# Moving the second layer's modulations out of the mixer, a transposed inverse, and six buffers in place of three

## The chip, the core and the metric

One core of a Trainium2 chip runs the whole program. The metric is the device time of one execution in microseconds (us); the time of a kernel is the median over its runs.

## What is computed

A backbone over 256 latent tokens and 256 context tokens of 1024 channels, with two layers. The first mixes tokens by a gated DeltaNet and differential attention, the second by a 2-D Fourier transform; each is followed by a PEER mixer (128 x 128 product keys, 16384 experts). Cut to what the change touches:

```
for i in range(DEPTH):                                        # DEPTH 2
    mod = (silu(c) @ ada_w[i] + ada_b[i]).reshape(bsz, 6, 1, D_MODEL)
    sh1, sc1, g1, sh2, sc2, g2 = (mod[:, j] for j in range(6))
    h = rmsnorm(x, norm1_w[i]) * (1.0 + sc1) + sh1
    if i % 2 == 0:
        y = mixer_ab(h, h_c, ...)   # h_c: the context, normalised and modulated alike
    else:
        y = fourier_mix(h) @ w_out_f[j]
    x = x + g1 * y
    x = x + g2 * peer(rmsnorm(x, norm2_w[i]) * (1.0 + sc2) + sh2, ...)
return rmsnorm(x, final_norm_w)

def gated_delta_chunked(...):      # in mixer_ab, per chunk of 64 tokens, head and direction
    m = where(strict, einsum('nbhid,nbhjd->nbhij', kb, kc) * decay, 0.0)
    t_inv = triangular_solve(eye + m, eye, lower=True, unit_diagonal=True)

def peer(h, w_q, sub_keys, u_tab, v_tab):
    ...                            # top 16 of the keys per head, softmax gates
    act = gelu(h . u_tab[idx]);  out = sum((gate * act) * v_tab[idx])
```

So layer 1's `mod` (six vectors of 1024, out of a 1024 x 6144 matrix) depends on `c` alone, and is first needed after peer 0.

## The kernel before

**The stages.** The mixer of layer 0 runs from the start to about 470 us, then peer 0, the Fourier layer, and peer 1 with the last norm. In the mixer, 29 products with the tiles of the input projection come first (17 of all 512 columns, context and latent tokens together, then 12 of the latent tokens' 256 columns), and each product's result is handed to a task (`do_k`, `do_ba`, `do_v`, `do_bk`, `do_bv`, `do_bq`, `do_q`, `do_gate`; list at L1318). The scalars of the DeltaNet (`do_ba` leads to `scalars`, L850, and `triangles`, L920) and the keys give 64 x 64 triangles `M`; `inverse` (L956) inverts the two diagonal 32 x 32 blocks of each, row by row, for 128 triangles at once (one on each partition). `blocks` (L1001) transposes the inverse `X` to the layout of the later steps, `merge` (L1029) adds the off-diagonal corner, `scan` runs the chunks in order. `attend` is the attention, in units of a score product, a softmax and a product with the values.

**The order.** `Lanes` (L50) records every instruction and plans it itself: the program is written as generators that yield at waits, a greedy planner keeps a cost for each operation (`took`, L98) and issues on each engine in the order in which the generators become ready. Each engine then runs its instructions strictly in that order. All instructions are therefore shown under one line, L133.

**Weights.** `Stream` (L200) carries all weight tiles of the program, 128 x 1024 f32 (512 KB) each, in one fixed order: `loads` (L214) issues them on SP's DMA queue into one of three `raw` buffers, and `cuts` (L225) splits a tile into two halves of reduced precision: ACT copies raw to `hi`, DVE computes `lo` = raw - hi. Buffers for the pairs are `pair` (two pairs), and, by stage, `wide` and `h` lent to the stream. `mm3` (L275) forms a product as hi.x_hi + hi.x_lo + lo.x_hi, 24 matmuls a tile. A matmul on f32 data shows as two records in the trace, one on the fp32r pairs as one.

**Peer.** 16 tiles of `wq`, 128 of `u` and 128 of `v`. While the first u tiles are multiplied, DVE selects the top keys and `weigh` (L1616) writes the gates; the u tiles after that and all v tiles have DVE and ACT for the cuts and for the splitting of the gated activations alone.

**Modulations.** `modulations` in the mixer (L579) goes over six parts (`parts`, L569), three of each layer, each of 16 chunks of `ada_w` (512 KB, `mraw` buffers, on SP's queue as well). A chunk's step is 4 matmuls (32 columns stationary, 256 moving, shown as 8 records); after each part a row copy, 4 transposes and one addition on DVE follow. Parts 0 to 2 are layer 0's, parts 3 to 5 layer 1's. `start` (L654) makes the modulated context and latent tokens: for each of 8 blocks POOL computes the context's `h` and the difference `h - hi`, DVE those of the latent tokens.

Of the kernel before, what the change touches and what calls it, by code (L numbers as in the profile page):

```python
# [9 lines left out]
F32 = mybir.dt.float32  # L10
# [4 lines left out]
OP = mybir.AluOpType  # L15
# [4 lines left out]
KC = 8  # L20
# [2 lines left out]
NEG = -3.0e38  # L23
GSC = 32768.0
SKEW = 16
AHEAD = 6
SUMMED = 6
LN_EXP = "natural_log_exp_and_others"
# [21 lines left out]
class Lanes:  # L50
# [149 lines left out]
class Stream:  # L200


    def __init__(self, c, pool, sources):
        self.c, self.n, self.sources = c, 0, sources
        lanes = c.nc
        self.raws = lanes.stock([c.t(pool, [128, 1024], tag=f"raw{i}") for i in range(3)])
# [18 lines left out]
    def cuts(self):  # L225
        for n in range(len(self.sources)):
            yield self.loaded[n]
            raw, t = self.raw.pop(n)
            hi = yield from self.parts[0].take()
            yield t  # L230
            self.c.nc.scalar.activation(hi, raw, AF.Copy)
            yield
            lo = yield from self.parts[1].take()
            self.tile[n] = hi, lo
            self.c.nc.vector.tensor_tensor(lo, raw, hi.bitcast(F32), op=OP.subtract)
            self.raws.give(raw)
            self.cut[n].set()
            yield

    def next(self):  # L240
        n = self.n
        self.n += 1
        yield self.cut[n]
        return self.tile.pop(n)
# [10 lines left out]
class Ctx:  # L255


    def __init__(self, tc, es, sources):
# [6 lines left out]
        self.stream = Stream(self, self.const, sources)  # L265

    def t(self, pool, shape, dt=F32, tag=None, **k):
        self.n += 1
# [269 lines left out]
def mixer(c, xT, aff, g1, coming, A):  # L538


    with ExitStack() as es:
# [24 lines left out]
        flight = lanes.stock(range(3))  # L566


        parts = [(i, p) for i in range(2) for p in range(3)]  # L569
        modk = events(len(parts))  # L570
        mrow = new([128, 512], tag="mrow")
        mraw = [new([128, 4, 256], tag=f"mraw{i}") for i in range(2)]
        mraw = [[view(S3, 4, 256, at=i * 1024) for i in range(4)] + mraw] + [mraw] * 5

        there = lanes.event()
        fetched = {n: lanes.event() for n in (6, 16)}
# [77 lines left out]
        def start():  # L654
# [21 lines left out]
            for n, k in enumerate(first):  # L676
                if n % 4 == 0:
                    yield mod0[n // 4]
                    (sc, shc), (s1, sh1) = (aff(r, n // 4) for r in (1, 0))
                for x, lo, eng, scale, shift in ((ctxT, 0, nc.gpsimd, sc, shc), (xT, NT, nc.vector, s1, sh1)):  # L680
                    hi = hb[:, 0, k, lo:lo + NT]
                    h = yield from hs.take()
                    nc.scalar.activation(hi, x[:, k], AF.Identity, scale=scale[:, k:k + 1], bias=shift[:, k:k + 1])
                    eng.tensor_scalar(h, x[:, k], scale[:, k:k + 1], shift[:, k:k + 1], op0=OP.mult, op1=OP.add)
                    eng.tensor_tensor(hb[:, 1, k, lo:lo + NT], h, hi.bitcast(F32), op=OP.subtract)
                    hs.give(h)
                hk[k].set()
            nc.gpsimd.memset(kbd, 0.0)
# [267 lines left out]
        def inverse():  # L956
            nc.gpsimd.memset(X, 0.0)
            nc.gpsimd.memset(S4[:, 0:4096:65], 1.0)
            yield
            Xb = [X[:, b * 32:b * 32 + 32, b * 32:b * 32 + 32] for b in range(2)]  # L960
            Mb = [M[:, b * 32:b * 32 + 32, b * 32:b * 32 + 32] for b in range(2)]
            for i in range(1, 32):
                for b in range(2):
                    nc.vector.tensor_tensor(pr[:, b, :i, :i], Mb[b][:, i, :i].unsqueeze(1).broadcast_to([128, i, i]),
                                            Xb[b][:, :i, :i].rearrange("p j x -> p x j"), op=OP.mult)
                for b in range(2):
                    nc.vector.tensor_reduce(Xb[b][:, i, :i], pr[:, b, :i, :i], axis=AX.X, op=OP.add)
                yield
            Xk.set()

# [30 lines left out]
        def blocks(d):  # L1001
            yield [Xk, zk]
            T = late["T"]
            ln = slice(d * 64, d * 64 + 64)
            for b in range(8):
                ps = yield from banks.take()
                pt = ps[:64].rearrange("p (x h u) -> p x h u", x=8, h=2)
                for a in range(8):
                    i = b * 8 + a
                    nc.tensor.transpose(pt[:, a], X[ln, :, i] if d else X[ln, i, :], c.ident[ln, ln])  # L1010
                yield
                for hp, q in halves():
# [302 lines left out]
                yield  # L1315


        tasks = [(do_k, p, 512) for p in range(4)] + [(do_ba, 0, 512)] + [(do_v, p, 512) for p in range(4)]  # L1318
        tasks += [(do_bk, p, 512) for p in range(4)] + [(do_bv, p, 512) for p in range(4)]
        tasks += [(do_bq, p, NT) for p in range(4)] + [(do_q, p, NT) for p in range(4)]  # L1320
        tasks += [(do_gate, p, NT) for p in range(4)]
# [74 lines left out]
def peer(c, layer, xT, shift, g2, coming, A):  # L1396
# [3 lines left out]
    with c.tc.tile_pool(name=f"peer{layer}", bufs=1) as dp:  # L1400
# [6 lines left out]
        a1 = c.t(dp, [128, 1024], F16, tag="a1")  # L1407
        x = c.scaled
        squares, c.squares = c.squares, Squares(c, layer == 0)
        late = {}  # L1410

        def region(j, n):
# [327 lines left out]
def trunk(tc, A, out):  # L1740
    with ExitStack() as es:
        tiles = lambda *names: [a[i] for a in names for i in range(a.shape[0])]
        layers = [tiles(A["wq"][i], A["u"][i], A["v"][i]) for i in range(2)]
        c = Ctx(tc, es, tiles(A["w_in"], A["w_out_ab"]) + layers[0] + [A["dft"]] + tiles(A["w_out_f"])
                + layers[1])
        nc = c.nc

        def const(name):
# [51 lines left out]
def arrays(i):  # L1800
# [17 lines left out]
    a["ada_w"] = con(i["ada_w"].reshape(2, 8, 128, 3, 4, 2, 256).transpose(0, 3, 5, 1, 2, 4, 6)).reshape(2, 3, 2, 8, 128, 1024)  # L1818
# [14 lines left out]
    a["w_in"] = np.concatenate([tiles(ak), tiles(ba), tiles(av), tiles(bk), tiles(bv), tiles(bq), tiles(aq), tiles(ag)])  # L1833
    a["conv"] = con(i["conv_w"][0].reshape(3, 12, 128).transpose(2, 1, 0))

    def lanes(x):
# [52 lines left out]
```

## Time and profile before

| what | value |
|---|---|
| runs | 2110.34, 2113.05 (median), 2118.28 us |
| profiled execution | 2115.18 us |
| its span | 2113.4 us |
| granted TensorE clock, mean | 0.989 |

The profile is of one execution. The span runs from the first to the last instruction of the trace. PE is the matmul engine and PEld its weight loads, DVE the vector engine, ACT the scalar engine, POOL GpSimd, SP the engine whose queue issues the loads. Names in rows are the program's: `S` holds the modulated tokens of the mixer, `bank` is a PSUM bank, `area` is shared storage of the mixer (`X` of the inverse lies in it), and `wide<-h,area` is the inverse's product row (`pr` in `wide`, `M` in `h`).

### The profile page before, as it was taken

What the parts mean: (1) busy time and instruction counts of PE and PEld (TensorE: products, weight loads), DVE (VectorE), ACT (ScalarE), POOL (GpSimd) and SP (SyncE); (2) the same over time, 40 slices, a digit from 0 to 9 for tenths busy, and PEclk for the clock granted to TensorE, in tenths of its full rate; (3) what the DMA queues carried; (4) which work ended last, traced back from release to release, by engine and by line L of the source; (5) the groups of instructions that cost most, each with busy time, mean ns of one, the idle gap of its engine ahead of it and who ended that gap; (6) DMA issues with size and microseconds to landing.
All of it is one profiled execution on the core that took longest, in us unless ns stands there. A gap on an engine that the chain in (4) does not pass through costs nothing.

```text
span 2113.4 us, 43065 instructions
## 1 busy us (share of the span) xinstructions
PE 2063.5 (98%) x17732; PEld 1933.9 (92%) x17732; DVE 1549.2 (73%) x3039; ACT 1022.1 (48%) x1542; POOL 82.8 (4%) x122
## 2 busy tenths in 40 slices
PE   7999989999999999999999999999999999999998
PEld 3566658989999999999999989999999999999997
DVE  3479978879998999565555556999899956555554
ACT  4443344155545444554444545554544455444453
POOL 3000023000000000000000000000000000000000
PEclk8999999999999999999999999999999999999999
DMA  7655671045565444665655543556544466666553
GB/s 300 213 180 169 232 240 38 1 133 180 189 198 170 142 149 151 198 212 196 192 195 194 193 160 116 172 190 199 170 141 149 150 199 211 195 194 193 196 192 118
DMA packets 102549, 370.65 MB, mean 175 GB/s; under 512 B 11696, under 2 KB 12976, under 8 KB 101968
## 3 DMA queue, kind: packets, MB, share of 16 engines
q1 hardware_dynamic: 102352, 367.90, 53.0%
q8 instruction: 138, 2.26, 0.4%
q14 instruction: 59, 0.48, 0.1%
HBM read 366.71 MB, written 1.15 MB: 174 GB/s over the span
## 4 chain that ended last, share of the span: by engine, by line
PE 79%; DVE 10%; DMA 6%; ACT 3%; issue 1%; POOL 0%; SPq 0%; POOLq 0%; ACTq 0%; DVEq 0%
PE bank L133 79%; DMA raw<-in_u_dram 3%; DVE wide_lo L133 3%; DVE pair L133 2%; DVE wide L133 2%; DMA mraw<-in_ada_w_dram 2%; DVE DD L133 1%; DVE area L133 1%; ACT pair L133 1%; DMA area<-in_ctx_dram 1%; ACT wide L133 0%; ACT DD L133 0%; DMA area<-in_ada_w_dram 0%; ACT bank L133 0%; DVE a L133 0%
## 5 line engine op out<-in xcount | busy, mean ns | idle before, releaser
L133 ACT ACTIVATE pair<-raw 128x1024 fp32r<-128x1024 f32 x376 | 399.1, 1062 | 435.2 <-PE bank L133 342.9
L133 DVE TENSOR_TENSOR pair<-raw,pair 128x1024 fp32r<-128x1024 f32 x376 | 458.1, 1219 | 182.8 <-ACT pair L133 167.1
L133 PE MATMUL bank<-h,pair 128*128 128x256 f32 x4464 | 557.4, 280 | 0.0
L133 PEld LDWEIGHTS bank<-h,pair 128*128 128x128 f32 x4464 | 528.8, 188 | 0.2 <-DVE pair L133 0.2
L133 PE MATMUL bank<-wide,pair 128*128 128x256 f32 (+1 forms) x3456 | 417.1, 277 | 0.0
L133 PEld LDWEIGHTS bank<-wide,pair 128*128 128x128 f32 x3456 | 405.4, 188 | 0.6
L133 PE MATMUL bank<-wide,h 128*128 128x256 f32 x2880 | 336.6, 276 | 0.0
L133 PEld LDWEIGHTS bank<-wide,h 128*128 128x128 f32 x2880 | 331.3, 188 | 0.0
L133 PE MATMUL bank<-h,wide 128*128 128x256 f32 x2160 | 264.5, 277 | 0.0
L133 PEld LDWEIGHTS bank<-h,wide 128*128 128x128 f32 x2160 | 253.7, 188 | 0.0
L133 DVE TENSOR_TENSOR h<-raw,h 128x1024 fp32r<-128x1024 f32 x120 | 147.0, 1225 | 140.1 <-ACT h L133 140.1
L133 ACT ACTIVATE h<-raw 128x1024 fp32r<-128x1024 f32 x120 | 127.4, 1062 | 161.8 <-PE bank L133 149.2
L133 PE MATMUL bank<-S,pair 128*128 128x256 f32 (+1 forms) x888 | 195.5, 362 | 4.2 <-POOL S L133 2.5
L133 PEld LDWEIGHTS bank<-S,pair 128*128 128x128 f32 x888 | 138.8, 199 | 52.3 <-issue 29.9
L133 ACT ACTIVATE DD<-bank 128x512 f32<-128x512 f32 (+25 forms) x284 | 107.6, 394 | 95.8 <-PE bank L133 92.8
L133 ACT ACTIVATE wide<-raw 128x1024 fp32r<-128x1024 f32 x90 | 95.6, 1062 | 106.7 <-PE bank L133 53.3
L133 DVE TENSOR_TENSOR wide<-raw,wide 128x1024 fp32r<-128x1024 f32 x90 | 109.3, 1214 | 2.3 <-ACT wide L133 2.0
L133 DVE TENSOR_TENSOR wide<-DD,wide 128x512 fp32r<-128x512 f32 x128 | 87.3, 684 | 8.3 <-ACT wide L133 8.2
L133 DVE TENSOR_TENSOR DD<-bank,DD 128x512 f32<-128x512 f32 (+13 forms) x84 | 42.3, 504 | 64.8 <-ACT bank L133 61.2
L133 DVE TENSOR_TENSOR wide_lo<-wide_lo,pT 128x1024 f16<-128x1024 f16 x128 | 85.9, 681 | 0.0
L133 ACT ACTIVATE wide<-DD 128x512 fp32r<-128x512 f32 x128 | 78.6, 615 | 9.5 <-PE bank L133 9.5
L133 POOL TENSOR_TENSOR wide_lo<-wide_lo 128x256 f32<-128x256 f32 x10 | 8.3, 834 | 1591.5 <-ACT wide_lo L133 1590.9
(242 smaller groups left out, 1893.7 us busy)
## 6 DMA issues: line engine op xcount, KB each, us to landing
raw<-in_u_dram SPq DMA_DIRECT2D x256, 512.0 KB, 3.5
raw<-in_v_dram SPq DMA_DIRECT2D x256, 512.0 KB, 4.3
mraw<-in_ada_w_dram SPq DMA_DIRECT2D x84, 512.0 KB, 4.2
raw<-in_wq_dram SPq DMA_DIRECT2D x32, 512.0 KB, 3.5
raw<-in_w_in_dram SPq DMA_DIRECT2D x29, 512.0 KB, 4.3
area<-in_ada_w_dram SPq DMA_DIRECT2D x12, 512.0 KB, 6.3
raw<-in_w_out_ab_dram SPq DMA_DIRECT2D x8, 512.0 KB, 4.5
raw<-in_w_out_f_dram SPq DMA_DIRECT2D x8, 512.0 KB, 3.5
```

Of the source, the lines that this page charges most:

```text
L133: return f(*args, **kw)
```

## The change

Five parts.

1. Layer 1's modulations leave the mixer: `parts` is three long there. Their 48 chunks, re-cut to 128 x 1024 (`ada_late`), go through the stream instead, one behind every third of the last 150 tiles of layer 0 (22 of u and all 128 of v of peer 0). DVE adds each chunk, scaled by the activated conditioning, into `acc`; after 8 chunks 8 matmuls with `acc` as the stationary operand and a column of ones as the moving one sum it over the partitions, and DVE adds the bias.
2. The stream has six raw buffers, not three, and the program a smaller scratch for DMA descriptors.
3. In `start`, the context's `h - hi` of the last four blocks goes from POOL to DVE.
4. `inverse` treats both 32 x 32 blocks in one operation, so it issues 31 products and 31 sums where it issued 62 and 62; X is kept transposed, so that the product reads X along adjacent elements instead of 64 elements (256 bytes) apart. `blocks` transposes the other one of its two cases.
5. `do_ba` is the first task, so the scalars come before the keys.

```
+RAW = 6
+ADA = 1, 0, 2, 4, 3, 5
 class Stream:
-        self.raws = lanes.stock([... for i in range(3)])
+        self.raws = lanes.stock([... for i in range(RAW)])
     def cuts(self):
             raw, t = self.raw.pop(n)
+            if n in self.sums:
+                yield from self.sum(raw, t, *self.sums[n])
+                continue
+    def sum(self, raw, t, m, k):
+        nc, w = self.c.nc, self.c.cact[:, k, 0:1]
+        if k == 0 and m != ADA[0]:
+            yield self.read[ADA[ADA.index(m) - 1]]
+        yield t
+        if k == 0:
+            nc.vector.tensor_scalar(self.acc, raw, w, None, op0=OP.mult)
+        else:
+            nc.vector.scalar_tensor_tensor(self.acc, raw, w, self.acc, op0=OP.mult, op1=OP.add)
+        self.raws.give(raw)
+        if k == KC - 1:
+            self.summed[m].set()
+        yield
+    def modulations(self):
+        for m in ADA:
+            yield self.summed[m]
+            ps = yield from c.banks.take()
+            for j in range(8):
+                nc.tensor.matmul(ps[:, j:j + 1], self.acc[:, j * 128:j * 128 + 128], c.ones[:, :1], start=True, stop=True)
+            self.read[m].set()
+            yield
+            nc.vector.tensor_tensor(c.mod[1][:, 0, m * 8:m * 8 + 8], ps[:, :8], c.adab[:, 1, m * 8:m * 8 + 8], op=OP.add)
+            c.banks.give(ps)
 def mixer(...):
-        parts = [(i, p) for i in range(2) for p in range(3)]
+        parts = [(0, p) for p in range(3)]
-        mraw = [[view(S3, 4, 256, at=i * 1024) for i in range(4)] + mraw] + [mraw] * 5
+        mraw = [[view(S3, 4, 256, at=i * 1024) for i in range(4)] + mraw] + [mraw] * 2
     def start():
-                    eng.tensor_tensor(hb[:, 1, k, lo:lo + NT], h, hi.bitcast(F32), op=OP.subtract)
+                    (eng if n < 4 else nc.vector).tensor_tensor(hb[:, 1, k, lo:lo + NT], h, hi.bitcast(F32), op=OP.subtract)
     def inverse():
-            for i in range(1, 32):
-                for b in range(2):
-                    nc.vector.tensor_tensor(pr[:, b, :i, :i], Mb[b][:, i, :i].unsqueeze(1).broadcast_to([128, i, i]),
-                                            Xb[b][:, :i, :i].rearrange("p j x -> p x j"), op=OP.mult)
-                for b in range(2):
-                    nc.vector.tensor_reduce(Xb[b][:, i, :i], pr[:, b, :i, :i], axis=AX.X, op=OP.add)
+            for i in range(1, 32):
+                x = both(X[:, 0, 0:1], [64, i], [1, i])
+                p = pr[:, :, :i, :i]
+                nc.vector.tensor_tensor(p, both(M[:, i, 0:1], [0, i], [1, i]), x, op=OP.mult)
+                nc.vector.tensor_reduce(both(X[:, 0, i:i + 1], [64, i]), p, axis=AX.X, op=OP.add)
     def blocks(d):
-                    nc.tensor.transpose(pt[:, a], X[ln, :, i] if d else X[ln, i, :], c.ident[ln, ln])
+                    nc.tensor.transpose(pt[:, a], X[ln, i, :] if d else X[ln, :, i], c.ident[ln, ln])
-        tasks = [(do_k, p, 512) for p in range(4)] + [(do_ba, 0, 512)] + [(do_v, p, 512) for p in range(4)]
+        tasks = [(do_ba, 0, 512)] + [(do_k, p, 512) for p in range(4)] + [(do_v, p, 512) for p in range(4)]
 def peer(c, layer, ...):
+        if layer == 0:
+            stream.acc = c.t(dp, [128, 1024], tag="acc")
+            lanes.add(stream.modulations())
 def trunk(tc, A, out):
+        chunks = [(m, k) for m in ADA for k in range(KC)]
+        sources, sums = tiles(A["w_in"], A["w_out_ab"]) + layers[0][:-150], {}
+        for j, v in enumerate(layers[0][-150:]):
+            sources.append(v)
+            while len(sums) < len(chunks) and j >= 3 * len(sums):
+                m, k = chunks[len(sums)]
+                sums[len(sources)] = m, k
+                sources.append(A["ada_late"][m, k])
 def kernel(**inputs):
+    nc = bacc.Bacc(..., dynamic_dma_scratch_size=1024)
```

`both(a, ...)` is an access pattern with a leading dimension of 2 blocks, 32 x 65 elements apart; the host's array of `w_in` tiles has the tile of `do_ba` first.

The planned order changes with it. **PE, the first narrow products of the mixer** (`S,pair` is a product with a tile of the input projection, `mraw,cact` a chunk's step, `area,bq` a score). Before:

```order
L133 MATMUL bank_4_67<-S_38_117,pair_15_78 128x256 x8
L133 MATMUL bank_3_66<-mraw_36_115,cact_88 32x256 x4
L133 MATMUL bank_8_71<-S_38_117,pair_12_75 128x256 x4
L133 MATMUL bank_5_68<-bq_120,later_138 128x256
L133 MATMUL bank_8_71<-S_38_117,pair_12_75 128x256 x4
L133 MATMUL bank_3_66<-mraw_37_116,cact_88 32x256 x4
L133 MATMUL bank_8_71<-S_38_117,pair_12_75 128x256 x8
L133 MATMUL bank_8_71<-S_38_117,pair_13_76 128x256 x8
L133 MATMUL bank_6_69<-area_28_107,bq_120 128x512
```

After:

```order
L135 MATMUL bank_1_64<-S_41_120,pair_18_81 128x256 x8
L135 MATMUL bank_6_69<-S_41_120,pair_15_78 128x256 x8
L135 MATMUL bank_5_68<-bq_123,later_141 128x256
L135 MATMUL bank_6_69<-S_41_120,pair_15_78 128x256 x8
L135 MATMUL bank_6_69<-S_41_120,pair_16_79 128x256 x8
L135 MATMUL bank_7_70<-S_41_120,pair_17_80 128x256 x4
L135 MATMUL bank_2_65<-bq_123,later_141 128x256
L135 MATMUL bank_7_70<-S_41_120,pair_17_80 128x256 x12
L135 MATMUL bank_7_70<-S_41_120,pair_18_81 128x256 x8
```

No step of a chunk stands between the products any more. By this order, 9 of layer 1's 48 steps stood among the wide products, 29 among the narrow ones and 10 behind them. Of the 16 score products 11 stood before the end of the narrow products and 5 behind; now it is 8 and 8.

**DVE, the end of the inverse** (`wide<-h,area` is the row product, `area<-wide` the sum, `sm`, `qT` and `bq` belong to the attention and the queries). Before:

```order
L133 TENSOR_REDUCE sm_136<-bank_3_66 128x1
L133 SCALAR_TENSOR_TENSOR area_31_110<-area_31_110,later_138 128x256
L133 TENSOR_SCALAR sm_136<-sm_136 128x1
L133 TENSOR_TENSOR wide_112<-h_111,area_29_108 128x31x31
L133 SCALAR_TENSOR_TENSOR area_31_110<-area_31_110,later_138 128x256
L133 TENSOR_TENSOR wide_112<-h_111,area_29_108 128x31x31
L133 TENSOR_REDUCE area_29_108<-wide_112 128x31 x2
L133 TENSOR_TENSOR pair_13_76<-raw_11_74,pair_12_75 128x1024
L133 TENSOR_REDUCE sm_136<-bank_4_67 128x1
```

After:

```order
L135 TENSOR_REDUCE sm_139<-bank_6_69 128x1
L135 TENSOR_SCALAR area_34_113<-area_34_113,later_141 128x256
L135 TENSOR_SCALAR sm_139<-sm_139 128x1
L135 TENSOR_TENSOR wide_115<-h_114,area_32_111 128x2x31x31
L135 SCALAR_TENSOR_TENSOR area_34_113<-area_34_113,later_141 128x256
L135 TENSOR_REDUCE area_32_111<-wide_115 128x2x31
L135 SCALAR_TENSOR_TENSOR area_34_113<-area_34_113,later_141 128x256
L135 TENSOR_TENSOR pair_18_81<-raw_14_77,pair_17_80 128x1024
```

Two products and two sums of a row became one of each, over both blocks; the rest of the queue around them is the same kind of work. Of the 29 cuts of the input projection's tiles, the 17th stood behind row 19 of the inverse and the 27th behind the last row, 31; now the 17th stands behind row 22 and the 24th behind row 31.

**PE, peer 0 where the value tiles begin** (`h,pair` is a product of a u tile, `wide,pair` one of a v tile). Before there were only these products here; in the change the first of six such groups stands among them:

```order
L135 MATMUL bank7_8_71<-h_73_3505,pair00_15_78 128x256 x16
L135 MATMUL bank7_8_71<-h_73_3505,pair01_16_79 128x256 x8
L135 MATMUL bank7_8_71<-h_73_3505,pair10_17_80 128x256 x8
L135 MATMUL bank5_6_69<-ones_22_87,acc_76_3508 128x1 x8
L135 MATMUL bank7_8_71<-h_73_3505,pair10_17_80 128x256 x8
L135 MATMUL bank7_8_71<-h_73_3505,pair11_18_81 128x256 x8
```

and on DVE, there, the bias addition (`mod1`) stands ahead of the next chunk's sum and the next cut:

```order
L135 TENSOR_TENSOR pair01_16_79<-raw3_12_75,pair00_15_78 128x1024
L135 TENSOR_TENSOR mod1_26_94<-bank5_6_69,early_20_83 128x8
L135 TENSOR_SCALAR acc_76_3508<-raw0_9_72,cact_24_91 128x1024
L135 SCALAR_TENSOR_TENSOR s11_79_12638<-mod1_26_94,early_20_83 128x8
L135 TENSOR_TENSOR pair11_18_81<-raw4_13_76,pair10_17_80 128x1024
```

The six groups are added; nothing was taken out of these two queues at this place.

## Rows read from the trace of the kernel before

**Rows 1.** The page, its busy times (part 1) and the chain that ended last (part 4).

```profile
PE 2063.5 (98%) x17732; PEld 1933.9 (92%) x17732; DVE 1549.2 (73%) x3039; ACT 1022.1 (48%) x1542; POOL 82.8 (4%) x122
...
PE 79%; DVE 10%; DMA 6%; ACT 3%; issue 1%; POOL 0%; SPq 0%; POOLq 0%; ACTq 0%; DVEq 0%
```

**Rows 2.** Windows: from:to, length, busy (x) of PE, PEld, DVE, ACT, POOL, clock, DMA, GB/s.

```profile
35.00:205.50 170.50, 166.94 (x1015) 106.41 (x1016) 115.81 (x252) 72.95 (x122) 20.12 (x16) 0.96 0.56 189
205.50:298.80 93.30, 85.23 (x619) 56.97 (x619) 78.30 (x138) 38.95 (x84) 11.43 (x14) 0.93 0.69 233
298.80:332.30 33.50, 29.36 (x290) 18.54 (x291) 29.39 (x61) 18.45 (x42) 10.51 (x2) 1.00 0.58 182
...
690.70:841.50 150.80, 148.57 (x1458) 144.80 (x1457) 143.36 (x227) 73.80 (x140) 0.00 (x0) 1.00 0.45 145
850.00:1240.00 390.00, 390.00 (x3440) 390.00 (x3439) 218.44 (x217) 192.12 (x218) 0.00 (x0) 1.00 0.60 194
```

**Rows 3.** Windows, tile mraw: PE, PEld busy, then clock, DMA, GB/s.

```profile
205.50:298.80 93.30, 19.41 (x232) 4.76 (x232) 0.93 0.69 233
298.80:332.30 33.50, 6.39 (x80) 1.57 (x80) 1.00 0.58 182
```

**Rows 4.** Timeline of PE in the mixer: start, duration, operation, [idle before <-releaser].

```profile
41.58 1.65 PE L133 MATMUL bank<-S,pair 128*128 128x512 f32 x3 [2.51 <-POOL S L133]
...
188.28 0.64 PE L133 MATMUL bank<-mraw,cact 128*32 128x256 f32 x8 [0.47 <-DMA mraw<-in_ada_w_dram]
...
203.19 0.64 PE L133 MATMUL bank<-mraw,cact 128*32 128x256 f32 x8
203.75 1.78 PE L133 MATMUL bank<-S,pair 128*128 128x512 f32 x9
...
276.72 1.08 PE L133 MATMUL bank<-mraw,cact 128*32 128x256 f32 x8 [2.53 <-DMA mraw<-in_ada_w_dram]
...
298.69 1.12 PE L133 MATMUL bank<-area,bq 64*128 64x512 f32 x2
```

**Rows 5.** DVE by line: all forms of the inverse's two operations, and single shapes.

```profile
L133 DVE TENSOR_TENSOR wide<-h,area 128x1 f32<-128x1 f32 (+30 forms) x62 | 44.8, 747 | 0.1
L133 DVE TENSOR_REDUCE area<-wide 128x1 f32<-128x1 f32 (+30 forms) x62 | 28.6, 491 | 0.0
...
L133 DVE TENSOR_TENSOR wide<-h,area 128x961 f32<-128x961 f32 x2 | 3.8, 1910 | 0.0
...
L133 DVE TENSOR_REDUCE area<-wide 128x31 f32<-128x961 f32 x2 | 2.2, 1180 | 0.0
```

**Rows 6.** DVE by line: a contiguous subtraction, and a scaled addition of 512 elements.

```profile
L133 DVE TENSOR_TENSOR pair<-raw,pair 128x1024 fp32r<-128x1024 f32 x376 | 458.1, 1219 | 182.8 <-ACT pair L133 167.1 <-PE bank L133 11.9 <-issue 3.5
...
L133 DVE SCALAR_TENSOR_TENSOR wide_lo<-wide_lo,sm 128x512 f32<-128x512 f32 x8 | 6.0, 747 | 0.1
```

**Rows 7.** Windows: the DMA engines at full load.

```profile
20.00:40.00 20.00, 15.45 (x102) 7.01 (x101) 12.58 (x34) 12.76 (x25) 11.78 (x14) 0.75 1.00 388
```

**Rows 8.** Timeline of PE: stationary 128 columns with few moving columns.

```profile
335.73 1.50 PE L133 MATMUL bank<-area 128*128 128x128 f32 x12
...
1265.95 0.50 PE L133 MATMUL bank<-ones,wide_lo 128*128 128x1 f32 x4
1266.32 0.48 PE L133 MATMUL bank<-pair,h 128*128 128x512 f32 x1
```

**Rows 9.** Waits in the stretch 690.7 to 841.5: who, for whom, us, times, longest.

```profile
ACT pair L133 <- DMA raw<-in_u_dram: 15.6, 13, 2.2
ACT wide L133 <- DMA raw<-in_u_dram: 13.9, 9, 2.8
DVE DD L133 <- ACT bank L133: 5.6, 10, 1.1
```

**Rows 10.** Timeline of PE: a u tile in peer 0 after the gates.

```profile
846.96 2.88 PE L133 MATMUL bank<-h,wide 128*128 128x256 f32 x24
849.68 5.60 PE L133 MATMUL bank<-h,pair 128*128 128x256 f32 x48
```

More of the change, by code (lines that the diff above doesn't have):

```diff
@@ L200, with __init__ @@
 class Stream:
-    def __init__(self, c, pool, sources):
-        self.c, self.n, self.sources = c, 0, sources
+    def __init__(self, c, pool, sources, sums):
+        self.c, self.n, self.sources, self.sums = c, 0, sources, sums
+        self.order = [n for n in range(len(sources)) if n not in sums]
+        self.acc, self.summed, self.read = None, c.nc.events(6), c.nc.events(6)
         lanes = c.nc
-        self.raws = lanes.stock([c.t(pool, [128, 1024], tag=f"raw{i}") for i in range(3)])
+        self.raws = lanes.stock([c.t(pool, [128, 1024], tag=f"raw{i}") for i in range(RAW)])
         self.parts = [lanes.stock(x) for x in zip(*(c.pair_tiles(pool, f"pair{i}") for i in range(2)))]
@@ L238, in cuts @@
             yield
+    def sum(self, raw, t, m, k):
[12 more added lines that the diff above has]
+    def modulations(self):
+        c, nc = self.c, self.c.nc
+        for m in ADA:
[7 more added lines that the diff above has]
+            c.banks.give(ps)
     def next(self):
-        n = self.n
+        n = self.order[self.n]
         self.n += 1
@@ L255, with __init__ @@
 class Ctx:
-    def __init__(self, tc, es, sources):
+    def __init__(self, tc, es, sources, sums):
         self.tc, self.nc = tc, Lanes(tc.nc)
@@ L264, in __init__ @@
         self.banks = self.nc.stock([self.t(banks, [128, 512], tag=f"bank{i}") for i in range(8)])
-        self.stream = Stream(self, self.const, sources)
+        self.stream = Stream(self, self.const, sources, sums)
     def t(self, pool, shape, dt=F32, tag=None, **k):
@@ L959, in inverse, with both @@
             yield
-            Xb = [X[:, b * 32:b * 32 + 32, b * 32:b * 32 + 32] for b in range(2)]
-            Mb = [M[:, b * 32:b * 32 + 32, b * 32:b * 32 + 32] for b in range(2)]
+            def both(a, *ap):
+                return bass.AP(tensor=a.tensor, offset=a.offset, ap=[a.ap[0], [32 * 65, 2], *ap])
             for i in range(1, 32):
-                for b in range(2):
-                    nc.vector.tensor_tensor(pr[:, b, :i, :i], Mb[b][:, i, :i].unsqueeze(1).broadcast_to([128, i, i]),
-                                            Xb[b][:, :i, :i].rearrange("p j x -> p x j"), op=OP.mult)
-                for b in range(2):
-                    nc.vector.tensor_reduce(Xb[b][:, i, :i], pr[:, b, :i, :i], axis=AX.X, op=OP.add)
+                x = both(X[:, 0, 0:1], [64, i], [1, i])
+                p = pr[:, :, :i, :i]
+                nc.vector.tensor_tensor(p, both(M[:, i, 0:1], [0, i], [1, i]), x, op=OP.mult)
+                nc.vector.tensor_reduce(both(X[:, 0, i:i + 1], [64, i]), p, axis=AX.X, op=OP.add)
                 yield
@@ L1743, in trunk @@
         layers = [tiles(A["wq"][i], A["u"][i], A["v"][i]) for i in range(2)]
-        c = Ctx(tc, es, tiles(A["w_in"], A["w_out_ab"]) + layers[0] + [A["dft"]] + tiles(A["w_out_f"])
-                + layers[1])
+        chunks = [(m, k) for m in ADA for k in range(KC)]
[6 more added lines that the diff above has]
+                sources.append(A["ada_late"][m, k])
+        c = Ctx(tc, es, sources + [A["dft"]] + tiles(A["w_out_f"]) + layers[1], sums)
         nc = c.nc
@@ L1816, in arrays @@
     a["cc"] = con(np.stack([i["c"][0], i["c_ctx"]], -1).reshape(8, 128, 2).transpose(1, 0, 2))
-    a["ada_w"] = con(i["ada_w"].reshape(2, 8, 128, 3, 4, 2, 256).transpose(0, 3, 5, 1, 2, 4, 6)).reshape(2, 3, 2, 8, 128, 1024)
+    a["ada_w"] = con(i["ada_w"][:1].reshape(1, 8, 128, 3, 4, 2, 256).transpose(0, 3, 5, 1, 2, 4, 6)).reshape(1, 3, 2, 8, 128, 1024)
+    a["ada_late"] = con(i["ada_w"][1].reshape(8, 128, 6, 1024).transpose(2, 0, 1, 3))
     a["ada_b"] = con(i["ada_b"].reshape(2, 48, 128).transpose(2, 0, 1))
@@ L1832, in arrays @@
     ba = np.concatenate([rows(bt), rows(al)] * 4, 1)
-    a["w_in"] = np.concatenate([tiles(ak), tiles(ba), tiles(av), tiles(bk), tiles(bv), tiles(bq), tiles(aq), tiles(ag)])
+    a["w_in"] = np.concatenate([tiles(ba), tiles(ak), tiles(av), tiles(bk), tiles(bv), tiles(bq), tiles(aq), tiles(ag)])
     a["conv"] = con(i["conv_w"][0].reshape(3, 12, 128).transpose(2, 1, 0))
@@ L1879 @@
     host = arrays({k: np.asarray(v) for k, v in inputs.items()})
-    nc = bacc.Bacc("TRN2", target_bir_lowering=False, num_devices=1)
+    nc = bacc.Bacc("TRN2", target_bir_lowering=False, num_devices=1, dynamic_dma_scratch_size=1024)
     A = {k: nc.dram_tensor(f"in_{k}_dram", v.shape, mybir.dt.from_np(v.dtype), kind="ExternalInput").ap()
```

## The prediction, made before the changed kernel ran

> **What bounds the kernel now.** I read the page first: PE is busy 98% of the span and the chain that ended last lies 79% on PE, 10% on DVE, 6% on DMA [rows 1]. So most of the program goes at PE's pace, and a gain is either PE work taken out or one of the few stretches in which PE waits. The windows by stage [rows 2] show them. In the plain u and v tiles of peer 0 (850 to 1240) PE is busy for all 390 us, DVE for 218, ACT for 192, and the loads run at 194 GB/s. In the stretch where the gates are written (690.7 to 841.5) DVE is busy 143.4 of 150.8 us and PE 148.6. In the mixer there are three stretches: the wide products (35 to 205.5, PE 166.9 of 170.5), the narrow ones (205.5 to 298.8, PE 85.2 of 93.3 at a clock of 0.93, DVE 78.3), and the rest of the attention up to the first merge (298.8 to 332.3, PE 29.4 of 33.5). Times are summed against the profiled execution, 2115.2 us; the median of the runs is 2.1 lower.
>
> **1. The chunks leave the mixer.** Of their 48 steps in layer 1, 9 stood among the wide products, 29 among the narrow ones, 10 behind. A step takes PE 0.57 us: 203.19 to the next product's start at 203.75 [rows 4]; the windows of this tile agree in count, 232 records for 29 steps of 8 and 80 for 10 [rows 3].
>
> *Wide products.* DVE is busy for 115.8 of 170.5 us there [rows 2], so what is added to it (four differences, of some 0.4 us, and the earlier inverse) is covered. PE's gain: 9 x 0.57 = 5.1, and most of one wait of 2.51 us on POOL's `S` at 41.58 [rows 4], since four differences leave POOL; that wait can give between 0 and 2.5, and I take 2, as POOL's own scalings ahead of it stay. With the wait of 0.47 us for a chunk at 188.28 [rows 4], **−7.5**.
>
> *Narrow products.* Here two engines have to give way at once. PE: 29 x 0.57 = 16.5, two groups of four transposes of a row (8 at 0.09, as the cheapest of rows 8: 0.7), one wait of 2.53 us for a chunk [rows 4], and three score products of 1.1 us each [rows 4], which now stand behind the last product: 3.3. That is 23. DVE: the inverse is 44.8 + 28.6 = 73.4 us in all [rows 5]. It computes 2 x (1 + 4 + ... + 961) = 20832 products; those of 961 took 1.91 us, that is 1.9 to 2.0 ns each, and their sum 1.18 us, 1.1 to 1.2 each [rows 5]. A cut, on adjacent elements, takes 1219 / 1024 = 1.19 ns [rows 6]. Reading X along adjacent elements, I put a product at 1.1 (that is 1.19 less the fixed part, some 0.08 us an instruction), a sum at 1.1 as before, and half as many fixed parts: 2 x 20832 x 1.1 ns = 46 and 62 x 0.08 = 5, 51 us in place of 73. Behind the 17th cut, DVE's order held the rows from 20 on, 15892 products at 1.9 + 1.1 ns and their fixed parts, some 50 us; it now holds those from 23 on, 13242 at 1.1 + 1.1, some 30. So DVE falls by about 20 and by 1 or 2 for softmaxes that move behind the products. The stretch follows the lesser of the two and keeps its idle time: **−22**.
>
> No row separates what X's stride costs from what the broadcast operand costs. From above it is 1.9 ns a product, the rate of rows 5; from below 1.1 as in rows 6; I take the latter, the same kind of operation on f32. [...]
>
> *Behind the products.* 10 x 0.57 = 5.7, four transposes 0.4, and about 1 of PE's 4.1 idle us [rows 2] are gone; the three score products come with 3.3 and what waits behind their softmaxes, of which I let 2 us show: **−2** (−7 to +8, the upper end with all of a unit's chain uncovered).
>
> **2. The chunks arrive in peer 0.** *PE.* 48 matmuls, 96 records, of 128 stationary columns and one moving column. The nearest rows: with one moving column 4 records took 0.37 us to the next start (1265.95 to 1266.32), 0.09 each; with 128 moving columns 12 took 1.50, 0.125 each [rows 8]. Between these, 0.11: 96 x 0.11 = 10.6 us (8.9 to 12.0), on the path, because PE is full there [rows 2]. The 48 steps taken away had cost 27. [...]
>
> *The first addition.* DVE's queue holds `mod1`, the next chunk's sum and then the next cut. `mod1` waits for the 16 records behind which PE has one more product half (16 matmuls, 1.8 us by rows 10) and a whole tile (2.72 us) before it needs that cut; DVE needs about 0.2 + 1.3 + 0.2 + 1.2 = 2.9. It can be late only when the cut's own ACT copy is: 0 to 1.4 us, and I take 1.4. The other five groups stand among v tiles with the same lead. Together **+12**.
>
> *DVE and DMA.* A sum of 1024 elements costs between 1.22 (the cut) and 1.49 us (twice 747) [rows 6]: 48 x 1.3 = 62 us, over 390 + 12 us of which DVE has 171 free [rows 2]. That cover fails only where DVE's lead over PE is used up. The loads: 48 more of 512 KB bring 194 to about 252 GB/s, and the queue has carried 388 for 20 us [rows 7]. Nothing.
>
> **3. Six raw buffers.** While the gates are written, ACT stands 15.6 + 13.9 = 29.5 us before `raw` loads that were issued too late, because a buffer comes free only when DVE has made the difference [rows 9]. Its queue then delays DVE (DVE waits for ACT 5.6 us in 10 pieces [rows 9]). DVE's 143.4 us of work is a floor, PE's own is lower: 42 tiles at 2.72 us [rows 10] and the transposes of the gates, some 142. With 150.8 us of time the gain is at most 7, at least nothing, if DVE's waits on ACT come from PE's results and not from the loads. I take 4, in the middle, and as the stretch comes in both peers, **−8** (0 to −14).
>
> **Sum.** −7.5 − 22 − 2 + 12 − 8 = −27.5; 2115.2 − 27.5 = 2087.7, and 2.1 lower for the median: **2086 us**, 1.3% faster.
>
> **Rivals.** A measurement of this kernel can tell a change of 0.5% (10.6 us) from none.
> - *A, the stride was not the price* (0.10). If products still cost 1.9 ns, DVE keeps 11 us in the narrow products, and the later start of what hangs on the inverse another 2 to 4: they gain some 8 instead of 22. Time: about 2100. For it: the broadcast operand remains; against: the contiguous cut.
> - *B, the attention's tail becomes the bound* (0.10). The score products moved behind the last product each start a chain over DVE and ACT; if these 8 units instead of 5 run without cover, the third stretch is 10 us longer instead of 2 shorter: about 2098.
> - *C, slower* (0.03). Each of the 48 sums stands ahead of a cut in DVE's queue. If the cuts are made just in time, each sum holds the next tile by its 1.3 us: +62 in place of nothing, 2148. It decides when DVE's lead is below one tile; against it stands the 44% of idle time of DVE while PE never waits [rows 2].
> - *D, more than I count* (0.09). The idle 8 us and the slow clock of the narrow products (0.93) both vanish, and both gate stretches reach DVE's floor: 2068.
> - *E, three buffers were enough* (inside the main case). ACT's waits turn out to be covered: 8 us less gain, 2094.
>
> **How the numbers follow.** The main case, 2074 to 2096, has 0.68: its bounds are 0 to −14 for the buffers and 8.9 to about 20 for peer 0. With A, B and D the range reaches 2066 to 2101; what lies outside is C, the worse half of A and the better half of D. Faster by over 0.5% is below 2102.5: the main case, B, D and most of A, 0.91; within 0.5%: 0.06; slower 0.03.
>
> **What would show it.** Among narrow products no wait for `mraw`, the stretch some 71 us long. One row product of the inverse over 2 x 961 elements near 2.1 us (A: 3.7). Peer 0's plain tiles 402 us long instead of 390, PE without idle time, 96 records of 0.1 us, and DVE 280 us busy (C: waits of PE for `pair`). The gate stretches near 147, with no wait of ACT for `raw`. The prediction is wrong if PE waits in peer 0 for DVE, or if the first merge does not come about 30 us earlier.

## The result and the profile after

The changed kernel's runs took 2086.86, 2089.08 and 2094.13 us, a median of 2089.08; those of the kernel before on the same chips have a median of 2115.66. The ratio is 0.9877 (95% interval 0.9856 to 0.9897), 1.2% faster, 26.6 us by the medians. The profiled execution took 2089.08 us, 26.1 less than that of before. (A fourth run, of 2527.46 us at a granted clock of 0.747, is left out.)

The page's busy times, against [rows 1]: PE lost 30 us of busy time and DVE gained 37.5.

```profile
PE 2033.6 (97%) x17432; PEld 1931.1 (93%) x17432; DVE 1586.7 (76%) x3032; ACT 1020.9 (49%) x1539; POOL 84.2 (4%) x118
```

Windows by stage, in the columns of [rows 2]: the wide products, the narrow ones, the rest up to the first merge, the stretch of the gates in peer 0. The last row is peer 0 from the same u tile as 860.6 in the kernel before to the first Fourier product; there that took 396.3 us.

```profile
36.00:194.40 158.40, 157.57 (x944) 104.23 (x945) 117.67 (x213) 73.34 (x122) 16.47 (x11) 0.99 0.53 179
194.40:258.60 64.20, 58.70 (x372) 47.11 (x372) 59.03 (x100) 34.27 (x75) 12.51 (x15) 0.95 0.38 115
258.60:293.40 34.80, 25.47 (x204) 16.76 (x200) 29.40 (x68) 18.76 (x46) 10.13 (x2) 0.80 0.05 16
...
651.30:798.50 147.20, 147.12 (x1458) 144.37 (x1457) 143.64 (x228) 75.09 (x141) 0.00 (x0) 1.00 0.46 150
...
817.60:1234.80 417.20, 409.99 (x3579) 407.99 (x3578) 274.58 (x283) 195.49 (x228) 0.73 (x1) 1.00 0.73 245
```

Laid side by side by the start of the same PE instructions in both traces, the difference is: up to the narrow products −11.5 us, the narrow products −29.2, behind them to the first merge +1.8, the rest of the mixer and the first u tiles −0.5, gates of peer 0 −3.6, peer 0 from there +20.9, the Fourier layer −1.0, gates of peer 1 −3.5; the rest is within 0.6. The sum is −26.2.

DVE by line, against [rows 5]: the inverse's products and sums, all forms and the largest.

```profile
L135 DVE TENSOR_TENSOR wide<-h,area 128x2 f32<-128x2 f32 (+30 forms) x31 | 26.5, 855 | 0.6
L135 DVE TENSOR_REDUCE area<-wide 128x2 f32<-128x2 f32 (+30 forms) x31 | 26.3, 849 | 0.5
...
L135 DVE TENSOR_TENSOR wide<-h,area 128x1922 f32<-128x1922 f32 x1 | 2.1, 2143 | 0.0
```

They take 52.8 us in place of 73.4. What is new in peer 0, by tile `acc`: counts, ns (least, median, most), first and last start, and what DVE waited for ahead of its sums (us, times, longest).

```profile
L135 PE MATMUL bank<-ones,acc x96: 164/250/271, 862.4 to 1208.3; 128*128 128x1 f32 x96
L135 DVE SCALAR_TENSOR_TENSOR acc<-raw,cact,acc x42: 1277/1284/1287, 812.1 to 1195.3; 128x1024 f32<-128x1024 f32 x42
L135 DVE TENSOR_SCALAR acc<-raw,cact x6: 743/744/754, 802.3 to 1139.7; 128x1024 f32<-128x1024 f32 x6
...
  DMA raw<-in_ada_late_dram: 83.8, 31
```

The waits of PE in that stretch, of which the kernel before had one of 0.9 us:

```profile
PE bank L135 <- DVE wide L135: 4.9, 5, 1.6
PE bank L135 <- ACT pair L135: 2.0, 2, 1.5
```

So DVE, free for a third of this stretch, stood 84 us before loads of chunks, and PE came to wait for tiles. The stretch is 20.9 us longer than before: PE is busy 14.6 us more in it, 11.1 of them the 96 new records, and idle 6.3 us more.

### The profile page after: what moved, and what is told of

The parts are those of the page before. It is cut to its first block, busy times and chain, and to the rows that moved or that the text cites. A ratio compares the mean times of both kernels' runs of the same rounds, so it can differ in the third digit from the quotient of the medians.

```text
span 2087.2 us, 42484 instructions
## 1 busy us (share of the span) xinstructions
PE 2033.6 (97%) x17432; PEld 1931.1 (93%) x17432; DVE 1586.7 (76%) x3032; ACT 1020.9 (49%) x1539; POOL 84.2 (4%) x118
## 5 line engine op out<-in xcount | busy, mean ns | idle before, releaser
L135 PE MATMUL bank<-wide,h 128*128 128x256 f32 x2904 | 342.4, 277 | 0.8 <-DVE wide L135 0.7
L135 PEld LDWEIGHTS bank<-wide,h 128*128 128x128 f32 x2904 | 335.7, 188 | 1.2 <-DVE wide L135 1.2
L135 PE MATMUL bank<-S,pair 128*128 128x256 f32 (+1 forms) x888 | 181.3, 349 | 6.1 <-DVE pair L135 4.1
L135 PEld LDWEIGHTS bank<-S,pair 128*128 128x128 f32 x888 | 132.8, 191 | 40.9 <-issue 18.5
L135 DVE SCALAR_TENSOR_TENSOR acc<-raw,cact,acc 128x1024 f32<-128x1024 f32 x42 | 53.9, 1284 | 83.9 <-DMA raw<-in_ada_late_dram 83.8
```

The costliest lines, as they stand in the source:

```text
L135: return f(*args, **kw)
```

## The experiments

Unless a median is given, a time is that of a single run. Such runs are compared by stage, through the start of the same PE instruction; the Fourier layer, where none of these kernels differ, took between 59.5 and 66.4 us, and what its share adds to a total is not an effect of the edit. The change's own times of a stage stand in brackets or as "in the change". No run moved the chunks alone, and none changed the scratch alone.

**1. Where the sums stand.** In the part of the program with the v tiles DVE's order is not the recorded one: there the framework's scheduler sorts it, and it moved the sums ahead of up to three cuts of tiles that are loaded before them (three by the order in which DVE starts them in the trace, where the expectations say four). A sum thus comes to the head of DVE's queue when its load has just been issued. The first try kept the recorded order of DVE for all of peer 0:

```
         with c.tc.manual_schedule(engines={mybir.EngineType.DVE}):
             lanes.run(uk[63])
+            if layer == 0:
+                lanes.run()
         lanes.run()
```

> The change, with DVE's order in peer 0's value stretch kept as recorded (the sums then stand in the order of the loads, not up to four tiles ahead). Theory (sums that run ahead stand at the head of DVE's queue before loads that have not landed, 84 us of waits, and hold the cuts behind them): those waits fall below 20 us, PE's waits for the v tiles' pairs (7 us) vanish, peer 0's stretch from the first u tile after the gates to the first Fourier product shrinks by 6 to 8 us, the whole is near 2082. Rival (48 sums are 58 us of DVE work and the loads go at 243 GB/s, wherever the sums stand): the same 7 us of PE waits remain, near 2089.

Measured: 2092.33 us; the stretch from the end of the first v tile to the first Fourier product took 365.0 us (365.8 in the change, 347.3 before). The waits for chunks and for `wide` were gone, and another wait had come: DVE 124.5 us, 60 times, for ACT's half of the split gates (`wide` there), which in this order block the rest. By its numbers the rival won, but the edit had replaced one wait by another, so it decides nothing between them. The next two moved the sums alone. Each sum became a task of its own and is issued on DVE behind the cut `last` (cut to these lines):

```
+                self.c.nc.add(self.sum(n, raw, t, *self.sums[n]), ground=True)
...
+        last = self.order[bisect.bisect(self.order, n) - 1 + LATE]
+        yield self.cut[last]
+        with self.c.tc.issue_after(self.made[last].ins):
             nc.vector.scalar_tensor_tensor(self.acc, raw, w, self.acc, op0=OP.mult, op1=OP.add)
```

LATE is 0:

> The change, with each sum issued on DVE behind the cut of the tile that was loaded before its chunk; the rest of the order is left to the scheduler as in the change. Theory (the sums that stand up to four tiles ahead of their place wait 84 us for loads at the head of DVE's queue and hold the cuts): DVE waits for the chunks' loads below 25 us in all, PE's waits for pairs in peer 0's value stretch go from 7 us to below 2, the stretch from the first v tile to the first Fourier product from 366 to about 358, the whole to about 2082. Rival (the order does not matter, the loads or DVE's added work cost it): 366 and 2089.

and 1:

> As the one before, but each sum behind the cut of one tile more, so that its load has had a tile's time longer. Theory: no waits of DVE for chunks at all (below 5 us), the value stretch 357 to 358 us: 347.3 as before the change, plus 9.3 for the five groups of matmuls that fall into it, plus 1. Rival (a raw buffer held a tile longer starves the loads behind it): ACT waits for raw loads, the stretch is 362 us or more.

Measured: 2082.69 and 2078.12 us, the stretch 357.5 and 357.1. No wait of DVE for a chunk is left among the waits of either. Windows of sums_after1, the same piece of peer 0 as the last window above: 408.0 us in place of 417.2, with the same DVE work and the same loads.

```profile
815.80:1223.80 408.00, 406.77 (x3579) 406.28 (x3579) 278.20 (x285) 196.03 (x229) 1.52 (x2) 1.00 0.77 250
```

The order of the sums cost 8 to 9 us; the rival, in which DVE's work or the loads cost it wherever the sums stand, is excluded: both are unchanged. The scatter of the stretch is smaller than that: in five kernels with the scheduler's order (the change and four of the edits below) it took 363.1 to 367.9 us, in four traces with the sums in their place 357.1 to 357.5. This is the version that beats both kernels, so it was timed.

> The same kernel as sums_after1, timed. Expected: a median of 2078 to 2084, a ratio to the kernel before of 0.980 to 0.985, where the change measured 0.9877 (0.9856 to 0.9897).

Measured: median 2078.8 (2076.47 to 2084.26), ratio 0.9822 (0.9806 to 0.9838), below the change's interval.

**2. The six buffers.** Three in the change:

```
-RAW = 6
+RAW = 3
```

> The change with three raw buffers. Theory (the buffers are worth the waits in the gate stretches alone): each gate stretch is about 4 us longer, ACT waits some 29 us for raw loads there again, the mixer is the same within 2 us, and in peer 0's value stretch the sums cannot run ahead by more than one tile; near 2095 in all. Rival (with 48 chunks more in the stream three buffers are too few in the value stretch): PE waits for tiles there by 10 us or more on top, near 2105 or above. Second rival (the buffers were worth nothing): 2089.

Measured: 2137.13 us, beside a run of the kernel before of 2122.36: in these single runs the change with three buffers is slower than no change. The gate stretch is 150.8 us again, with the old waits, but the v tiles' stretch is 396.0 us. Waits in raw3, 652 to 803 us:

```profile
ACT wide L135 <- DMA raw<-in_u_dram: 15.0, 11, 2.5
ACT pair L135 <- DMA raw<-in_u_dram: 12.5, 13, 2.5
```

and among the v tiles, 882 to 1277 us, where PE waits for what ACT, held up by loads, then delivers late:

```profile
ACT pair L135 <- DMA raw<-in_v_dram: 107.6, 46, 5.4
ACT h L135 <- DMA raw<-in_v_dram: 84.4, 39, 4.2
...
PE bank L135 <- ACT wide L135: 10.3, 16, 2.2
```

My theory of their worth had only the gate stretches in it, and fell. Whether this was again the order was tried with three buffers and the sums in their place (sums_after0 with `RAW = 3`):

> Three raw buffers with each sum behind the cut of the tile loaded before its chunk. Theory (three buffers are too few for four loads in the time of three tiles, whatever the order): the value stretch of peer 0 stays above 385 us (396.0 with the order of the change), near 2130. Rival (it was the sums' order that cost so much with three buffers too): 357 to 365 us, near 2095.

Measured: 2109.61 us, the stretch 369.9 us: between the two. Of the 38.5 us between 396.0 and sums_after0's 357.5, the order makes 26.1 and the number of buffers 12.4, if the order is mended first; with the buffers first they make 30.2 (396.0 to 365.8) and the order 8.3. The two act together, so neither has a price of its own. Then the buffers, in the kernel before (with the smaller scratch for DMA descriptors, as in the change):

```
-        self.raws = lanes.stock([... for i in range(3)])
+        self.raws = lanes.stock([... for i in range(6)])
```

> The kernel before with six raw buffers and nothing else. Theory: each gate stretch 3.6 to 4.3 us shorter (146.9 and 139.6 from 150.8 and 144), ACT's waits for raw loads there gone, the mixer within 2 us, near 2107 where the kernel before has 2115 on the same chip: 8 us less than the kernel before beside it. Rival (buffers fill earlier and collide with the chunks' loads in the mixer): the mixer some 3 us longer, the gain below 5.

Measured: 2116.15 us, 2.3 less than the run of the kernel before beside it. Both gate stretches fell by about 3.6 us, as expected (before_raw6, 691 to 838):

```profile
691.00:838.00 147.00, 146.91 (x1450) 144.21 (x1449) 143.46 (x229) 75.49 (x139) 0.00 (x0) 1.00 0.47 150
```

but the mixer was 3.4 us longer. PE's waits there (34 to 338 us) had been 4.7 us for chunks before:

```profile
PE bank L133 <- DMA mraw<-in_ada_w_dram: 11.7, 11, 4.2
PE bank L133 <- POOL S L133: 3.3, 1, 3.3
```

The longer waits fit the rival, in which tiles loaded early push the chunks back in the same queue. They are not the whole account: two waits of PE for DVE, 6.5 us together, are gone from this mixer, and behind the narrow products the granted clock is 0.82 in place of 1.00. In these single runs neither the buffers without the removal of the chunks nor the removal without the buffers shortened the program by more than the runs scatter.

**3. The inverse.** Undone in the change, with the transposes of before:

```
-                nc.vector.tensor_tensor(p, both(M[:, i, 0:1], [0, i], [1, i]), x, op=OP.mult)
-                nc.vector.tensor_reduce(both(X[:, 0, i:i + 1], [64, i]), p, axis=AX.X, op=OP.add)
+                for b in range(2):
+                    nc.vector.tensor_tensor(pr[:, b, :i, :i], ..., Xb[b][:, :i, :i].rearrange("p j x -> p x j"), op=OP.mult)
+                for b in range(2):
+                    nc.vector.tensor_reduce(Xb[b][:, i, :i], pr[:, b, :i, :i], axis=AX.X, op=OP.add)
```

> The change with the inverse of before: 62 row products and 62 sums, X not transposed. Theory (DVE is the second bound of the narrow products, and the inverse gave it some 20 us): the narrow products take 10 to 16 us longer (64 becomes 74 to 80), near 2102 in all. Rival (the stretch is PE's, and the chunks that left it are the whole gain): the narrow products take at most 3 us longer, near 2091.

Measured: 2106.35 us; narrow products 79.5 us (64.5), behind them 31.4 (35.6): together 10.8 longer. The theory holds for the narrow products, less what the tail gives back. Then one operation for both blocks, but X read as before:

```
-                x = both(X[:, 0, 0:1], [64, i], [1, i])
+                x = both(X[:, 0, 0:1], [1, i], [64, i])
-                nc.vector.tensor_reduce(both(X[:, 0, i:i + 1], [64, i]), p, ...)
+                nc.vector.tensor_reduce(both(X[:, i, 0:1], [1, i]), p, ...)
```

> The change with one operation for both blocks but X kept as before, so that the product reads X 256 bytes apart. Theory (the stride is the price): a row product of 1922 elements takes 3.5 to 3.8 us in place of 2.14, all 31 some 42 us in place of 26.5; the sums stay at 26; the narrow products are 8 to 12 us longer, near 2099. Rival (fewer instructions are the gain, the stride costs nothing): 2.1 to 2.3 us a product, 2089 as the change.

Measured: 2104.48 us, narrow products 79.1 (14.6 more, where 8 to 12 were expected), behind them 37.5. DVE by line in inv_strided:

```profile
L135 DVE TENSOR_TENSOR wide<-h,area 128x2 f32<-128x2 f32 (+30 forms) x31 | 41.8, 1349 | 0.6
L135 DVE TENSOR_REDUCE area<-wide 128x2 f32<-128x2 f32 (+30 forms) x31 | 26.3, 847 | 0.5
...
L135 DVE TENSOR_TENSOR wide<-h,area 128x1922 f32<-128x1922 f32 x1 | 3.5, 3457 | 0.0
```

The same 31 products, on the same elements, cost 41.8 us in place of 26.5: the stride costs 15.3 us, the broadcast operand nothing that shows. Half as many instructions saved the rest, 2.6 us of products and 2.3 of sums (44.4 and 28.6 in inv_old). Yet inv_strided, with 5 us less work on DVE, reached the merge 5.7 us later than inv_old. The difference lies behind the narrow products, in a DVE scaling beside a clearing on POOL (part 5 below) and in PE's wait, inv_strided first, then inv_old:

```profile
273.85 5.65 DVE L135 TENSOR_SCALAR bq<-bq,later 128x256 f32<-128x256 f32 x1
281.14 4.88 PE L135 MATMUL bank<-area,bq 64*128 64x512 f32 x6 [6.91 <-DVE gate L135]
```

```profile
276.10 3.52 DVE L135 TENSOR_SCALAR bq<-bq,later 128x256 f32<-128x256 f32 x1
280.54 2.07 PE L135 MATMUL bank<-area,bq 64*128 64x512 f32 x2 [2.97 <-ACT wide_lo L135]
```

PE's wait makes 3.9 us of it; the rest goes with the clock, 0.73 in the mean of that stretch against 0.84. An edit of the narrow products is therefore not to be judged by their stretch alone.

**4. The order of tasks, and POOL.** `do_k` first (and its tiles):

```
-        tasks = [(do_ba, 0, 512)] + [(do_k, p, 512) for p in range(4)] + ...
+        tasks = [(do_k, p, 512) for p in range(4)] + [(do_ba, 0, 512)] + ...
```

> The change with the keys' products first and do_ba fifth, as before. Theory (the early scalars let the inverse start earlier and spread it over the wide products): the narrow products and the attention behind them up to the first merge take 5 to 10 us longer than the 100.1 us of the change, near 2096. Rival (DVE has room either way once the inverse is cheaper): within 2 us, 2089.

Measured: 2094.17 us; narrow products and tail 102.2 us, 2.1 more, the wide ones 2.0 more. The rival is nearer: the early scalars are worth some 4 us here, less than the 5 to 10 of the theory. All of the context's differences on POOL:

```
-                    (eng if n < 4 else nc.vector).tensor_tensor(hb[:, 1, k, lo:lo + NT], ...)
+                    eng.tensor_tensor(hb[:, 1, k, lo:lo + NT], ...)
```

> The change with all eight of the context's differences on POOL, as before. Theory: PE waits 2 to 3 us on POOL for the last blocks of the first product, the wide products take that much longer, 2091. Rival (with the scalars' tile first PE finds other work): no change within 1 us.

Measured: 2102.95 us. PE waited 2.8 us for POOL at 42.1, as expected, but the wide products took 6.8 us longer, not 3. The window behind the wait in pool_diff shows the rest, a granted clock of 0.50. In the kernel before a chunk's step took 0.57 us to the next start at a clock of 1.00 [rows 4] and 1.02 at 0.50 (220.81 to 221.83). Counted by the clock, 6.8 us at 0.50 hold some 3.4 us of work, an estimate:

```profile
42.20:49.00 6.80, 6.80 (x17) 4.93 (x18) 0.16 (x1) 0.47 (x3) 5.38 (x4) 0.50 0.48 191
```

**5. The tail of the attention.** In the change PE stands 6.9 us for one operation of DVE. Timeline of the change there, POOL, DVE, then PE:

```profile
258.16 6.92 POOL L135 MEMSET S<- 128x8192 f32 x1 [2.43 <-PE bank L135]
```

```profile
258.44 1.22 DVE L135 TENSOR_TENSOR pair<-raw,pair 128x1024 fp32r<-128x1024 f32 x1
259.58 5.65 DVE L135 TENSOR_SCALAR bq<-bq,later 128x256 f32<-128x256 f32 x1
265.15 0.41 DVE L135 TENSOR_TENSOR bq<-bq,rt 128x256 f32<-128x256 f32 x1
...
266.08 0.34 DVE L135 TENSOR_SCALAR bq<-bq,later 128x256 f32<-128x256 f32 x1
```

```profile
266.87 4.88 PE L135 MATMUL bank<-area,bq 64*128 64x512 f32 x6 [6.91 <-DVE gate L135]
```

The scaling that takes 0.34 us at 266.08 took 5.65 at 259.58 and ended when POOL's clearing did. A plain two-input operation beside the same clearing was not slowed (1.22 us at 258.44, and 1219 ns in the mean of [rows 6]), nor was a scaling of one column beside that of the kernel before (0.14 us at 301.71, and 0.13 at 306.01, behind the clearing). In five other traces (the kernel before, inv_old, inv_strided, k_first, pool_diff) a wide scaling that started beside the clearing ends 0.1 to 0.3 us behind it as well, whenever it started: it took 1.00 us in k_first, 3.52 in inv_old, 3.72 in the kernel before. By what means the clearing holds the scaling, no trace shows; that shorter pieces would let it in between was my guess. So the clearing was cut into 16, on top of sums_after1:

```
-            nc.gpsimd.memset(late["T"], 0.0)
+            for d in range(2):
+                for u in range(0, 32, 4):
+                    nc.gpsimd.memset(late["T"][:, d, u:u + 4], 0.0)
```

> sums_after1 with POOL's one clearing of 8192 elements (6.92 us, behind the last input product) cut into 16 clearings of 512. Theory (a DVE scaling of 256 elements took 5.65 us in place of 0.34 because it could not run beside that clearing; PE then waited 6.9 us and its clock was halved for 13.7 us): no DVE scaling there takes over 1.5 us, PE's wait is below 3 us, the stretch from the last input product to the first merge goes from 35.6 to 26 to 31 us, the whole to 2069 to 2075. Rival (the pieces follow each other closely enough to hold DVE just as long): the same 5 to 6 us in one DVE operation, 35 us, 2079.

Measured: median 2083.48, ratio 0.9844 (0.9821 to 0.9867); the stretch to the merge 40.0 us (35.6 in sums_after1), so nothing was gained. The rival won (timelines of memset_split, POOL and DVE):

```profile
258.00 7.51 POOL L137 MEMSET S<- 128x512 f32 x16 [2.43 <-PE bank L137]
```

```profile
259.42 6.24 DVE L137 TENSOR_SCALAR bq<-bq,later 128x256 f32<-128x256 f32 x1
```

DVE got in between none of the pieces that were left. That the pair of operations collides is shown by the durations (5.65 and 6.24 us against 0.34); the reason was not shown, and what the tail would take without the collision was not measured.

## Why the prediction was right, and where it was not

The time fell where it was forecast (26.1 us by the profiled executions, 27.5 in the sum), but that the sum came so near is luck: the wide and narrow products gave 11.2 us more than their terms, the tail and peer 0 took 12.7 us more than theirs, and these errors cancelled. By the prediction's own signs it was wrong in peer 0, where PE waits 4.9 us for DVE, and right in the mixer, where the first merge came 38.9 us earlier.

- *Wide products, −7.5: −11.5.* Nine steps and the POOL wait went as counted. What was missing is the clock around that wait: the granted clock was 0.50 from 30.0 to 47.0 us in the kernel before, and only from 36.5 to 39.9 in the change. Of the wide products 9.6 us of PE's busy time lay in the first stretch and 3.4 in the second; at 0.50 that is some 3 us more work lost before (an estimate). pool_diff brings the wait back, and 6.8 us with it. In the kernel before the clock had gone to 0.50 at 30.0, 9 us ahead of the wait, so the wait did not set it off there; what did is not shown. Windows, the kernel before first:

```profile
30.00:47.00 17.00, 13.14 (x48) 7.47 (x41) 8.31 (x21) 8.60 (x18) 16.80 (x16) 0.50 0.69 257
```

```profile
36.50:39.90 3.40, 3.40 (x10) 2.62 (x9) 3.09 (x7) 3.40 (x7) 3.40 (x4) 0.50 1.02 418
```

- *Narrow products, −22: −29.2.* Both engines gave way: PE is busy 58.7 us (85.2) and DVE 59.0 (78.3), the 20 us of DVE as worked out. The step that failed is "follows the lesser of the two and keeps its idle time": DVE gave 19.3 us of work and 9.8 of its 15.0 idle, so the stretch fell by more than DVE's work. PE's term of 23, of which 2.5 was a wait, had its idle time right (2.6 less) and its work too small: 26.5 us in place of 20.5. Here too the clock was left out. In the kernel before, it went to 0.50 twice for 6.8 us, once at a wait of 4.04 us for DVE and once at the wait of 2.53 us for a chunk [rows 4]; in the change it did so once, at a wait of 2.45 us. That is some 3.4 us of PE's 6.0 (an estimate from these windows); the rest is open. inv_old shows that without the inverse's share some 15 us of this stretch would have been lost again. Windows, the kernel before twice, then the change:

```profile
217.70:224.50 6.80, 6.80 (x29) 3.61 (x29) 5.36 (x8) 0.78 (x2) 0.00 (x0) 0.50 0.59 208
275.70:282.50 6.80, 5.78 (x30) 4.97 (x31) 3.58 (x11) 3.05 (x7) 3.09 (x9) 0.51 0.74 257
```

```profile
227.60:234.40 6.80, 6.33 (x19) 3.97 (x20) 6.38 (x16) 3.11 (x8) 1.79 (x1) 0.50 0.96 248
```

- *The price of a product, 1.1 ns, and of the last row, 2.1 us:* 2.143 us measured. Rival A is out, by inv_strided: the stride was the price, 15.3 us on 20832 products, 0.73 ns each. That the 1.1 ns of a cut [rows 6] would hold for the product too was an estimate; why the stride costs this much is not shown.
- *Behind the products, −2: +1.8.* Rival B's direction, by another mechanism as far as the traces show: of PE's 9.3 idle us there, 6.9 are one wait behind a DVE operation that POOL's clearing held, and the clock fell to 0.80 in the mean, where it had been 1.00.
- *Peer 0, +12: +20.9.* This is the term that failed most. The 96 records took 11.1 us of PE, some 0.12 each, and a sum 1.28 us, both as bounded. The step that failed is "Nothing" for DVE and DMA: I took the cover by its total (171 free us, 388 GB/s), and not by who stands at the head of DVE's queue. That is rival C's place with another price: not 1.3 us a sum, but the wait for its load. With the sums in their place, the same piece takes 408.0 us, +11.7: the forecast's number, now with its mechanism, but for the first addition.
- *The first addition, 1.4 us:* DVE's additions of the bias waited 6.8 us in all for PE, 6 times; behind the first of them, at 864 us, PE runs on without a wait. Zero would have been right.
- *Six buffers, −8: −7.1,* in both peers, and ACT's waits for u loads are gone there. But the buffers carried more than the term said: with three, the change took 48 us more (2137.13 against 2089.08, single runs) and was slower than the kernel before. Slower, as in rival C, would then have been the result, though by waits of ACT and DVE for loads; that outcome was nearer than 3 in 100 suggests.

## What to carry to other kernels

Work that is put on an engine with much free time still costs what stands behind it in that engine's queue: look up where the scheduler puts it and when its load lands, and tie it behind work of its own time (9 us here, by the order alone). A buffer count that looks generous for the old stream is part of the price of a longer stream: try the change with the old count before booking the buffers as a gain of their own. And behind a short wait of PE the clock can be slower: in pool_diff 6.8 us at 0.50 followed a wait of 2.8 us. It need not: behind a wait of 2.52 us at 307.25 in the kernel before the clock stayed at 1.00 ([rows 2], 298.8 to 332.3).

## What was not expected of the hardware

One clearing on POOL held a DVE scaling for 5.65 us in place of 0.34, and 16 pieces of it held it for 6.24; the kernel before has the same collision (3.72 us, a scaling of 512 elements at 302.37). And the clock behind such a wait: windows of the change, the wait and the stretch after it.

```profile
258.60:265.20 6.60, 1.36 (x8) 0.30 (x4) 6.60 (x3) 1.13 (x4) 6.48 (x1) 1.00 0.22 79
265.20:278.80 13.60, 11.10 (x28) 5.62 (x29) 10.38 (x34) 5.21 (x14) 0.00 (x0) 0.50 0.01 1
```

PE was busy 1.36 of 6.6 us at a granted clock of 1.00, and then had 0.50 for the 13.6 us that followed, while it was already busy again for 11.10 of them; in memset_split, behind a wait of 7.5 us, it was 23.9 us at 0.50.
